# First two channel blocks multiplied one token stream at a time, and the last 512 output columns handled in halves

## The chip, the cores and the metric

One Trainium2 chip, one of its cores. The metric is the device time of the whole kernel in microseconds (us). Five engines work side by side, each through its own instructions in the order in which they stand: TensorE (PE in the rows; PEld is its weight load), VectorE (DVE), ScalarE (ACT), GpSimd (POOL) and SyncE (SP), which here only issues DMAs. They wait for each other through semaphores.

## The reference

Two layers of a token mixer with two streams of 256 tokens each and 1024 channels: the latent tokens `x`, and the context tokens `ctx`. Each layer has a gated FFN, a mixer and a second FFN; every one takes a modulated input and ends with a post-norm. Cut to what matters here:

```python
def _modulate(x, shift, scale):
    return _ln(x) * (1.0 + scale) + shift

def _swiglu(u, w_gate, w_up, w_down):
    return (jax.nn.silu(u @ w_gate) * (u @ w_up)) @ w_down
...
        mod = jax.nn.silu(c) @ w_mod[l] + b_mod[l]
        mod_c = jax.nn.silu(c_ctx) @ w_mod[l] + b_mod[l]
...
        h = _post_norm(h, 0.5 * m[2] * _swiglu(_modulate(h, m[0], m[1]), ...), ln_g[l, 0], ln_b[l, 0])
...
    return h
```

The output is the stream `h` of the latent tokens alone, after the last FFN of the second layer.

## The kernel before, in words

Tokens stand in four tiles of 128: tiles 0 and 1 are the first stream (latent tokens), tiles 2 and 3 the second (context tokens). Channels stand in eight blocks of 128, numbered `j`. Every matrix product is made in three passes of split float32 (`mm3`: high by high, high by low, low by high), so each weight tile has a part `whi` (cast by ScalarE, L68) and a part `wlo` (subtracted by VectorE, L69), and each input block has `uhi` and `ulo`.

The program begins in `run` with the first FFN of layer 0, whose first two weight tiles are multiplied while the inputs are still being made:

- `norm(t)` loads token tile `t`, takes its statistics on VectorE (`bn`, L190, and a few small instructions, one of them a power on GpSimd, L197) and normalises it on ScalarE into `xn` (L211).
- `mod_first(j)` loads the modulation weights of block `j` in two DMAs of 512 KB (`wm`, L112), multiplies them on TensorE in two halves of four matmuls (`pm`, L115; the trace counts each twice), copies the product on ScalarE (`msb`, L118), transposes it (`pmt`, L122), and VectorE makes shift and scale from it (`mred`, `modT`).
- `modulate_first(j)` transposes block `j` of all four token tiles (`put`, L134), applies shift and scale on ScalarE, one instruction a stream (`uv`, L138), and VectorE splits it into `uhi` (L140) and `ulo` (L141).
- `gate(j)` makes 12 matmuls of 512 columns (two weight tiles, gate and up, three passes), which add block `j` into four PSUM tiles. After `gate(7)` the same FFN goes on with its third weight tile.

A scheduler decides the order of each engine's instructions when the program is built; the order that it chose is fixed in the program. All these loads go through SyncE's one queue, in its order.

The program ends in `ffn(1, 1)` for the two tiles of the first stream. For its last 512 output columns, tile by tile: 33 matmuls (`pd`, eleven hidden blocks by three passes), `evac` on VectorE (multiply by the gate `ev` L259, add to `h` L264, statistics L190), and `boundary`: aggregate the statistics, the power on GpSimd (L197), subtract mean and scale (L275), scale and shift (L276), and one DMA of 512 KB to the output on SyncE's queue (L278).

Of the kernel before, what the change touches and what calls it, by code (L numbers as in the profile page):

```python
# [14 lines left out]
D = 1024  # L15
# [11 lines left out]
class Kernel:  # L27
# [45 lines left out]
    def mm3(self, ps, a, b, start, stop):  # L73
        """ps += a^T b, with a, b (high, low) pairs."""
        mm = self.nc.tensor.matmul
        mm(ps, a[0], b[0], start=start, stop=False)  # L76
        mm(ps, a[0], b[1], start=False, stop=False)  # L77
        mm(ps, a[1], b[0], start=False, stop=stop)  # L78

    # ---------------------------------------------------------------- set-up  # L80
# [24 lines left out]
    def mod_first(self, j, pool):  # L105
        """Shift and scale of model channels 128 j .. 128 j + 127 in the first sub-layer."""
# [22 lines left out]
    def modulate_first(self, j, pool, xn):  # L129
        """u of model channels 128 j .. 128 j + 127, all tokens."""  # L130
        nc = self.nc
        pt = self.psd.tile([128, 512], F32, name="put", tag="d")
        for t in range(4):
            nc.tensor.transpose(pt[:, 128 * t:128 * t + 128], xn[t][:, 128 * j:128 * j + 128], self.ident)  # L134
        v = pool.tile([128, 512], F32, name="uv", tag="uv", bufs=2)
        for s in range(2):
# [3 lines left out]
        nc.vector.tensor_copy(self.uhi[:, j], v)  # L140
        nc.vector.tensor_sub(self.ulo[:, j], v, self.uhi[:, j].bitcast(F32))  # L141
# [22 lines left out]
    def mod(self, l, n):  # L164
        """Columns 512 n .. 512 n + 511 of both streams' modulation vectors of layer l, 128 (on partitions) a step."""
# [19 lines left out]
    # ---------------------------------------------------------------- norms  # L185
    def bn(self, tt, ch):
        """Partial statistics of half a row of h."""
        if ch == 0 or tt not in self.bst:
            self.bst[tt] = self.sm.tile([128, 2, 6], F32, name="bst", tag="bst")
        self.nc.vector.bn_stats(self.bst[tt][:, ch], self.h[:, tt, 512 * ch:512 * ch + 512])  # L190

    def rsqrt(self, var, scale):
        """(var * scale + eps) ** -0.5"""
# [6 lines left out]
    def row_stats(self, tt):  # L200
        mv = self.sm.tile([128, 2], F32, name="mv", tag="mv")
        self.nc.vector.bn_aggr(mv, self.bst.pop(tt))
# [11 lines left out]
    def modulate(self, pool, l, slot, tt, xn, gs=(0, 1), dve=0):  # L214
        """u (feature-major, high and low) = xn (1 + scale) + shift for one token tile."""
# [20 lines left out]
    def load_gate(self, pool, l, gate, streams):  # L236
        """The gates of a sub-layer, on every partition."""
# [7 lines left out]
    def load_norm(self, pool, l, i):  # L245
        """Row vectors of a post-norm, on every partition."""
# [7 lines left out]
    def evac(self, pool, nrm, tt, ch, ps, first, final):  # L254
        """h += gate * ps on one half of the columns (h scaled by alpha at the first)."""
        nc = self.nc
        cs = slice(512 * ch, 512 * ch + 512)
        t = pool.tile([128, 512], F32, name="ev", tag="ev", bufs=2)
        nc.vector.tensor_mul(t, ps, nrm[TT_S[tt]][:, cs])  # L259
# [5 lines left out]
        if final:  # L265
            self.bn(tt, ch)

    def boundary(self, pool, nrm, tt, nxt):
        """h = LN(h) g + b; then the next sub-layer's modulated input, or the output."""
# [5 lines left out]
        nc.vector.scalar_tensor_tensor(xn, h, mu, nrm["g"], op0=OP.subtract, op1=OP.mult)  # L275
        nc.vector.scalar_tensor_tensor(h, xn, rs, nrm["b"], op0=OP.mult, op1=OP.add, accum_out=q[:, 0:1])  # L276
        if nxt is None:
            nc.sync.dma_start(self.out[128 * tt:128 * tt + 128], h)  # L278
            return
# [4 lines left out]
    # ---------------------------------------------------------------- FFN  # L284
    def ffn(self, l, f, tiles, nxt, mid, begun=None, post=()):
        """mid(stack): for each half of the hidden channels, streams (steps, from, to) to run in the places
        0 to 22 between the weight tiles; begun: the PSUM tiles of the first two weight tiles, if they are already done."""
# [3 lines left out]
        with ExitStack() as es:  # L291
# [6 lines left out]
            for fh in range(2):  # L298
# [29 lines left out]
                for ch in range(2):  # L328
# [5 lines left out]
                    def step(k, t):  # L334
                        i = tiles.index(t)
                        hi, lo = ws[k]
                        self.mm3(ps[t], (gt[k][:, 0, 128 * i:128 * i + 128], gt[k][:, 1, 128 * i:128 * i + 128]),
                                 (hi, lo), start=k == 0, stop=k == 10)
# [32 lines left out]
    def gate_load(self, l, f, ms, outer=False):  # L371
        """Weights (one pair per half of the model channels) and PSUM tiles of hidden tiles ms."""
# [19 lines left out]
    def gate_out(self, pool, PS, T):  # L392
        """silu(u w_gate) (u w_up), feature-major, high and low parts."""
# [948 lines left out]
```

## Time and profile before

| | |
|---|---|
| time, median of 3 runs | 2058.04 us (2054.61 to 2058.64) |
| span of the profiled execution | 2059.9 us, from the first to the last instruction |
| TensorE busy | 1980.4 us, 96% of the span |
| VectorE busy | 1519.5 us, 74% |
| ScalarE busy | 781.1 us, 38% |
| mean granted TensorE clock | 0.987 |

The profiled execution has no time of its own beside its span; the span is 1.9 us above the median of the three runs. Busy times are sums over the whole program, which has stages with different limits; the change touches only the first 60 us and the last 20 us, so these are read by themselves.

### The profile page before, as it was taken

To read this page: it belongs to the slowest core of one execution; us is meant where nothing else is said; L and a number is where in the kernel's file an instruction comes from. 1 tells how busy PE (TensorE), PEld (TensorE's weight loads), DVE (VectorE), ACT (ScalarE), POOL (GpSimd) and SP (SyncE) were. 2 spreads that over 40 slices of the span, in tenths; PEclk is the share of its full clock that TensorE was granted. 3 is DMA by queue.
4 is the path that set the end of the run, shared out by engine and by line. 5 is a ranking of instruction groups with operands and counts; after the bars stand their busy time and mean duration, and the time that the engine had idled before them with its cause. 6 is when DMAs were issued, how large, how long until landed. Compare 5 with 4: busy or idle time off the path is not lost. (4 is left out here: it accounts for less than half of the span.)

```text
span 2059.9 us, 28737 instructions
## 1 busy us (share of the span) xinstructions
PE 1980.4 (96%) x10556; PEld 1644.6 (80%) x10556; DVE 1519.5 (74%) x3352; ACT 781.1 (38%) x1300; POOL 157.0 (8%) x221
## 2 busy tenths in 40 slices
PE   7999999999999999999999989999998999979997
PEld 4888887787767887888888878888887877968896
DVE  4996998868996347766998767768778587684555
ACT  4321332345554224432233252312224566444442
POOL 0000110121100002200000030000003110010000
PEclk9999999999999999999999999999999999998999
DMA  8454566355344333345565525546552643564563
GB/s 312 154 152 143 184 202 215 118 178 163 120 147 133 101 103 123 113 148 180 184 197 186 187 97 188 166 158 198 173 183 88 188 156 117 163 232 136 182 188 112
DMA packets 103119, 333.10 MB, mean 162 GB/s; under 512 B 12353, under 2 KB 25505, under 8 KB 102977
## 3 DMA queue, kind: packets, MB, share of 16 engines
q1 hardware_dynamic: 96384, 310.96, 47.6%
q10 hardware_dynamic: 3584, 14.24, 1.8%
q0 software_dynamic: 3008, 6.07, 1.0%
q8 instruction: 83, 1.36, 0.3%
q14 instruction: 60, 0.48, 0.1%
HBM read 313.70 MB, written 17.51 MB: 161 GB/s over the span
## 5 line engine op out<-in xcount | busy, mean ns | idle before, releaser
L68 ACT CAST whi<-raw 128x1024 fp32r<-128x1024 f32 (+1 forms) x384 | 394.9, 1031 | 615.6 <-PE pd L78 160.2
L69 DVE TENSOR_TENSOR wlo<-raw,whi 128x1024 fp32r<-128x1024 f32 (+1 forms) x384 | 462.7, 1207 | 219.8 <-ACT whi L68 218.3
L178 DVE SCALAR_TENSOR_TENSOR pj<-raw,cb 128x512 f32<-128x512 f32 x512 | 351.7, 706 | 51.3 <-DMA raw<-in_w_modT 47.7
L76 PE MATMUL pg<-uhi,whi 128*128 128x512 f32 (+1 forms) x736 | 265.7, 361 | 1.6 <-DVE uhi L233 1.3
L78 PE MATMUL pg<-uhi,wlo 128*128 128x512 f32 (+1 forms) x736 | 263.1, 357 | 2.3 <-DVE wlo L69 2.3
L76 PE MATMUL pu<-uhi,whi 128*128 128x512 f32 (+1 forms) x736 | 263.2, 358 | 1.5 <-DVE ev L259 1.5
L77 PE MATMUL pg<-ulo,whi 128*128 128x512 f32 (+1 forms) x736 | 263.2, 358 | 0.6 <-POOL ulo L234 0.5
L77 PE MATMUL pu<-ulo,whi 128*128 128x512 f32 (+1 forms) x736 | 262.7, 357 | 0.0
L78 PE MATMUL pu<-uhi,wlo 128*128 128x512 f32 (+1 forms) x736 | 262.5, 357 | 0.0
L77 PE MATMUL pd<-wlo,gT 128*128 128x512 f32 x616 | 240.6, 391 | 1.6 <-DVE wlo L69 1.5
L76 PE MATMUL pd<-whi,gT 128*128 128x512 f32 x616 | 240.8, 391 | 0.9 <-DVE ev L259 0.9
L78 PE MATMUL pd<-whi,gT 128*128 128x512 f32 x616 | 239.5, 390 | 0.0
L76 PEld LDWEIGHTS pg<-uhi,whi 128*128 128x128 f32 x736 | 140.9, 191 | 26.1 <-issue 3.8
L78 PEld LDWEIGHTS pg<-uhi,wlo 128*128 128x128 f32 x736 | 140.7, 191 | 22.0 <-DVE wlo L69 2.7
L76 PEld LDWEIGHTS pu<-uhi,whi 128*128 128x128 f32 x736 | 140.9, 192 | 21.6 <-DVE ev L259 1.7
L77 PEld LDWEIGHTS pg<-ulo,whi 128*128 128x128 f32 x736 | 140.4, 191 | 20.9 <-POOL ulo L234 1.1
L77 PEld LDWEIGHTS pu<-ulo,whi 128*128 128x128 f32 x736 | 140.6, 191 | 20.2 <-issue 0.8
L78 PEld LDWEIGHTS pu<-uhi,wlo 128*128 128x128 f32 x736 | 140.5, 191 | 19.8 <-issue 0.4
L76 PEld LDWEIGHTS pd<-whi,gT 128*128 128x128 f32 x616 | 115.6, 188 | 27.2 <-issue 1.3
L77 PEld LDWEIGHTS pd<-wlo,gT 128*128 128x128 f32 x616 | 115.7, 188 | 25.9 <-DVE wlo L69 2.5
L78 PEld LDWEIGHTS pd<-whi,gT 128*128 128x128 f32 x616 | 115.7, 188 | 23.9
L76 PE MATMUL pgg<-uhi,whi 128*128 128x512 f32 (+1 forms) x384 | 131.8, 344 | 0.0
(561 smaller groups left out, 3234.0 us busy)
## 6 DMA issues: line engine op xcount, KB each, us to landing
raw<-in_w_gu SPq DMA_DIRECT2D x176, 512.0 KB
raw<-in_w_modT SPq DMA_DIRECT2D x128, 512.0 KB
raw<-in_w_dn SPq DMA_DIRECT2D x80, 512.0 KB
raw<-in_w_in SPq DMA_DIRECT2D x80, 512.0 KB
sd<-sst ACTq DMA_DIRECT2D x16, 802.0 KB
sst<-sd SPq DMA_DIRECT2D x16, 802.0 KB
wm<-in_w_mod SPq DMA_DIRECT2D x16, 512.0 KB
raw<-in_w_br SPq DMA_DIRECT2D x16, 512.0 KB
```

The lines of the kernel that those rows point to most:

```text
L68: nc.scalar.copy(hi[:, :m], raw[:, :m])
L69: nc.vector.tensor_sub(lo[:, :m], raw[:, :m], hi[:, :m].bitcast(F32))
L76: mm(ps, a[0], b[0], start=start, stop=False)
L77: mm(ps, a[0], b[1], start=False, stop=False)
L78: mm(ps, a[1], b[0], start=False, stop=stop)
L178: V.scalar_tensor_tensor(junk, raw[:, 512 * k:512 * k + 512], 1.0, self.cb[:, s, 512 * k:512 * k + 512], op0=OP.mult, op1=OP.mult, accum_o ...
```

## The change

At the start, `modulate_first` can work on one stream, and `gate` on half of the columns. Blocks 0 and 1 are made and multiplied for the first stream (256 columns) with only token tiles 0 and 1; the loads and norms of tiles 2 and 3 come after the first weight tiles and after the modulation weights of block 1; then blocks 0 and 1 are made and multiplied for the second stream, behind `begun`. From block 2 on all 512 columns go together, and the modulation of a block runs one block further ahead. At the end, the last token tile's last 512 columns are made in two halves of 33 matmuls of 256 columns each, each half is evacuated by itself, and every output tile is scaled and stored in two halves, the first on ScalarE's DMA queue and the second on SyncE's. Comments and docstrings are removed besides. The core of the diff:

```diff
-    def modulate_first(self, j, pool, xn):
+    def modulate_first(self, j, pool, xn, streams=(0, 1)):
...
-        v = pool.tile([128, 512], F32, name="uv", tag="uv", bufs=2)
-        for s in range(2):
+        v = pool.tile([128, 512], F32, name="uv", tag="uv", bufs=3)
+        for s in streams:
+            for t in range(2 * s, 2 * s + 2):
+                nc.tensor.transpose(pt[:, 128 * t:128 * t + 128], xn[t][:, 128 * j:128 * j + 128], self.ident)
...
         xn = pool.tile([128, D], F32, name="xn1", tag="xn", bufs=2)
...
+        if nxt is None:
+            for i, eng in enumerate((nc.scalar, nc.sync)):
+                cs = slice(512 * i, 512 * i + 512)
+                nc.vector.scalar_tensor_tensor(h[:, cs], xn[:, cs], rs, nrm["b"][:, cs], op0=OP.mult, op1=OP.add)
+                eng.dma_start(self.out[128 * tt:128 * tt + 128, cs], h[:, cs])
+            return
         nc.vector.scalar_tensor_tensor(h, xn, rs, nrm["b"], op0=OP.mult, op1=OP.add, accum_out=q[:, 0:1])
-        if nxt is None:
-            nc.sync.dma_start(self.out[128 * tt:128 * tt + 128], h)
-            return
...
                     for t in tiles:
-                        for k in range(11):
-                            step(k, t)
-                        self.evac(pool, nrm, t, ch, ps[t], False, True)
+                        if nxt is None and t == tiles[-1]:
+                            for i in range(2):
+                                for k in range(11):
+                                    step(k, t, 256 * i, 256 * i + 256)
+                                self.evac(pool, nrm, t, ch, ps[t], False, True, (i,))
+                        else:
+                            for k in range(11):
+                                step(k, t)
+                            self.evac(pool, nrm, t, ch, ps[t], False, True)
...
                 xn = [norm(t) for t in range(2)]
                 next(mod[0])
-                xn += [norm(t) for t in range(2, 4)]
                 next(mod[0], None)
-                self.modulate_first(0, pool, xn)
                 load(0)
                 next(mod[1])
+                self.modulate_first(0, pool, xn, (0,))
                 next(mod[1], None)
-                for j in range(KT):
-                    if j == 1:
-                        load(1)
-                    if j + 1 < KT:
-                        self.modulate_first(j + 1, pool, xn)
+                xn += [norm(t) for t in range(2, 4)]
+                begun = gate(0, 0, 256)
+                self.modulate_first(1, pool, xn, (0,))
+                next(mod[2])
+                gate(1, 0, 256)
+                next(mod[2], None)
+                for j in range(2):
+                    self.modulate_first(j, pool, xn, (1,))
+                for j in range(2):
+                    with self.tc.issue_after(begun):
+                        gate(j, 256, 512)
+                    self.modulate_first(j + 2, pool, xn)
+                    next(mod[j + 3])
+                    next(mod[j + 3], None)
+                load(1)
+                for j in range(2, KT):
...
```

Three places of the built programs, where the prediction's terms rest. Outside the first eight blocks and the last output columns every engine's order is the same in both.

ScalarE near the start, before: `xn` are the normalised token tiles (the first row holds tiles 0 and 1), `msb` the copied modulation products, `whi` weight casts, `uv` the modulated blocks.

```order
L211 ACTIVATE xn<-h,nb,nv 128x1024 x2
L118 COPY msb<-pm 128x256
L211 ACTIVATE xn<-h,nb,nv 128x1024
L68 CAST whi<-raw 128x1024
L211 ACTIVATE xn<-h,nb,nv 128x1024
L68 CAST whi<-raw 128x1024
L138 ACTIVATE uv<-put,modT 128x256 x2
L118 COPY msb<-pm 128x256
```

The same place now:

```order
L216 ACTIVATE xn<-h,nb,nv 128x1024 x2
L118 COPY msb<-pm 128x256
L68 CAST whi<-raw 128x1024 x2
L138 ACTIVATE uv<-put,modT 128x256
L118 COPY msb<-pm 128x256
L138 ACTIVATE uv<-put,modT 128x256
L216 ACTIVATE xn<-h,nb,nv 128x1024 x2
L118 COPY msb<-pm 128x256
L138 ACTIVATE uv<-put,modT 128x256 x4
```

The norms of tiles 2 and 3 moved behind the first stream's `uv` of blocks 0 and 1, and the copy `msb` of block 2 stands behind them.

VectorE near the start, before: `bst`, `mv`, `nv`, `nmu`, `nb` are a token tile's statistics, the last two norms (tiles 2 and 3) stand here.

```order
L190 BN_STATS bst<-h 128x6
L210 TENSOR_TENSOR nb<-nmu,nv 128x1
L190 BN_STATS bst<-h 128x6
L126 TENSOR_SCALAR modT<-mred,bmT 128x2
L202 BN_AGGR mv<-bst 128x2
L196 TENSOR_SCALAR nv<-mv 128x1
L1178 TENSOR_SCALAR nmu<-mv 128x1
L210 TENSOR_TENSOR nb<-nmu,nv 128x1
L69 TENSOR_TENSOR wlo<-raw,whi 128x1024 x2
L140 CAST uhi<-uv 128x512
L141 TENSOR_TENSOR ulo<-uv,uhi 128x512
```

The same place now, from the statistics of tile 2 on; `uhi` and `ulo` here are block 1 of the first stream:

```order
L192 BN_STATS bst<-h 128x6 x2
L141 CAST uhi<-uv 128x256
L207 BN_AGGR mv<-bst 128x2
L192 BN_STATS bst<-h 128x6
L200 TENSOR_SCALAR nv<-mv 128x1
L1193 TENSOR_SCALAR nmu<-mv 128x1
L192 BN_STATS bst<-h 128x6
L215 TENSOR_TENSOR nb<-nmu,nv 128x1
L142 TENSOR_TENSOR ulo<-uv,uhi 128x256
L207 BN_AGGR mv<-bst 128x2
L200 TENSOR_SCALAR nv<-mv 128x1
L1193 TENSOR_SCALAR nmu<-mv 128x1
```

The rest of both norms moved behind `uhi` of block 1, and between `uhi` and `ulo` of that block now stand eight instructions of the norms.

VectorE at the very end, before: the last token tile's evacuation and post-norm.

```order
L259 TENSOR_TENSOR ev<-pd,gbc_17304 128x512
L264 TENSOR_TENSOR h<-h,ev 128x512
L190 BN_STATS bst<-h 128x6
L202 BN_AGGR mv<-bst 128x2
L196 TENSOR_SCALAR nv<-mv 128x1
L275 SCALAR_TENSOR_TENSOR xn_18448<-h,mv,lng 128x1024
L276 SCALAR_TENSOR_TENSOR h,q<-xn_18448,nv,lnb 128x1024
```

The same place now:

```order
L265 TENSOR_TENSOR ev<-pd,gbc_17336 128x256
L270 TENSOR_TENSOR h<-h,ev 128x256
L192 BN_STATS bst<-h 128x6
L265 TENSOR_TENSOR ev<-pd,gbc_17336 128x256
L270 TENSOR_TENSOR h<-h,ev 128x256
L192 BN_STATS bst<-h 128x6
L207 BN_AGGR mv<-bst 128x2
L200 TENSOR_SCALAR nv<-mv 128x1
L281 SCALAR_TENSOR_TENSOR xn_18519<-h,mv,lng 128x1024
L285 SCALAR_TENSOR_TENSOR h<-xn_18519,nv,lnb 128x512 x2
```

Each instruction of the evacuation is there twice at half the width, and the last one of the post-norm is cut in two.

## Rows read from the trace of the kernel before

**Rows 1.** The page, busy time of the engine, share of the span, instructions.

```profile
PE 1980.4 (96%) x10556; PEld 1644.6 (80%) x10556; DVE 1519.5 (74%) x3352; ACT 781.1 (38%) x1300; POOL 157.0 (8%) x221
```

**Rows 2.** Timeline of TensorE, the start: start us, us, engine, line, operation, count.

```profile
18.09 1.94 PE L115 MATMUL pm<-wm,cTs 128*32 128x256 f32 x16
20.21 0.80 PE L76 MATMUL pg<-uhi,whi 128*128 128x512 f32 x1 [0.19 <-DVE uhi L140]
...
30.12 0.39 PE L76 MATMUL pg<-uhi,whi 128*128 128x512 f32 x1
30.35 0.39 PE L77 MATMUL pg<-ulo,whi 128*128 128x512 f32 x1
...
56.23 0.39 PE L76 MATMUL pg<-uhi,whi 128*128 128x512 f32 x1
```

**Rows 3.** Timeline of TensorE, one block's modulation among the products.

```profile
36.10 0.38 PE L122 MATMUL pmt<-ident,msb 128*128 128x128 f32 x2
...
36.85 0.64 PE L115 MATMUL pm<-wm,cTs 128*32 128x256 f32 x8
37.42 0.50 PE L77 MATMUL pg<-ulo,whi 128*128 128x512 f32 x1
37.76 0.39 PE L78 MATMUL pg<-uhi,wlo 128*128 128x512 f32 x1
```

**Rows 4.** Timeline of VectorE, the start.

```profile
6.22 1.29 DVE L190 BATCH_NORM_STATS2 bst<-h 128x6 f32<-128x512 f32 x2 [4.78 <-DMA h<-in_hx]
...
10.29 0.16 DVE L210 TENSOR_TENSOR nb<-nmu,nv 128x1 f32<-128x1 f32 x1 [0.60 <-POOL nv L197]
11.33 1.29 DVE L190 BATCH_NORM_STATS2 bst<-h 128x6 f32<-128x512 f32 x2 [0.89 <-DMA h<-in_hx]
```

**Rows 5.** Stretches 14 to 18 us: length, busy PE, PEld, DVE, ACT, POOL, PEclk, DMA, GB/s.

```profile
14.00:16.00 2.00, 0.39 (x1) 0.18 (x1) 1.36 (x8) 1.69 (x2) 0.63 (x2) 1.00 1.04 317
16.00:18.00 2.00, 0.40 (x2) 0.18 (x1) 1.36 (x2) 2.00 (x3) 0.00 (x0) 1.00 1.01 412
```

**Rows 6.** Groups of instructions, 0 to 60 us, by form: busy us, mean ns, idle before.

```profile
L138 ACT ACTIVATE uv<-put,modT 128x256 f32<-128x256 f32 x16 | 8.2, 560 | 12.3 <-DVE modT L126 12.3
...
L211 ACT ACTIVATE xn<-h,nb,nv 128x1024 f32<-128x1024 f32 x4 | 4.9, 1236 | 8.3 <-DVE nb L210 8.3
...
L118 ACT COPY msb<-pm 128x256 f32<-128x256 f32 x8 | 2.9, 369 | 6.3 <-PE pm L115 6.3
```

**Rows 7.** Timeline of TensorE, matmuls of 256 columns around a change of clock.

```profile
1864.27 0.41 PE L78 MATMUL pg<-uhi,wlo 128*128 128x256 f32 x1
1864.49 0.41 PE L76 MATMUL pu<-uhi,whi 128*128 128x256 f32 x1
...
1865.12 0.28 PE L77 MATMUL pg<-ulo,whi 128*128 128x256 f32 x1
1865.24 0.28 PE L78 MATMUL pg<-uhi,wlo 128*128 128x256 f32 x1
```

**Rows 8.** Timeline of VectorE, the end.

```profile
2049.41 0.69 DVE L259 TENSOR_TENSOR ev<-pd,gbc 128x512 f32<-128x512 f32 x1 [1.97 <-PE pd L78]
...
2050.86 0.69 DVE L190 BATCH_NORM_STATS2 bst<-h 128x6 f32<-128x512 f32 x1
...
2053.62 1.28 DVE L276 SCALAR_TENSOR_TENSOR h<-xn,nv,lnb 128x1024 f32<-128x1024 f32 x1 [0.44 <-POOL nv L197]
```

**Rows 9.** Timeline of GpSimd, the end.

```profile
2052.07 1.52 POOL L197 TENSOR_TENSOR nv<-nv,mhalf 128x1 f32<-128x1 f32 x1 [5.96 <-DVE nv L196]
```

**Rows 10.** Groups of instructions, 1975 to 2060 us, by form.

```profile
L398 DVE TENSOR_TENSOR sg<-sg,pu 128x256 f32<-128x256 f32 x8 | 3.4, 421 | 6.1 <-ACT sg L397 6.1
```

**Rows 11.** One stretch of the output's transfer, columns as in rows 5.

```profile
2056.00:2057.00 1.00, 0.00 (x0) 0.00 (x0) 0.00 (x0) 0.00 (x0) 0.00 (x0) 0.50 1.00 410
```

**Rows 12.** Two stretches with a fall of TensorE's clock, columns as in rows 5.

```profile
308.00:311.77 3.77, 1.59 (x7) 0.97 (x6) 3.77 (x11) 0.00 (x0) 1.03 (x2) 1.00 0.50 150
311.77:315.18 3.41, 3.32 (x8) 2.64 (x9) 3.27 (x10) 1.55 (x2) 0.00 (x0) 0.50 0.77 225
```

More of the change, by code (lines that the diff above doesn't have):

```diff
@@ L77, in mm3 @@
         mm(ps, a[0], b[1], start=False, stop=False)
-        mm(ps, a[1], b[0], start=False, stop=stop)
+        self.last = mm(ps, a[1], b[0], start=False, stop=stop)
     def setup(self, pool):
@@ L139, in modulate_first @@
                                  scale=self.modT[0][:, 8 + j, s:s + 1])
-        nc.vector.tensor_copy(self.uhi[:, j], v)
-        nc.vector.tensor_sub(self.ulo[:, j], v, self.uhi[:, j].bitcast(F32))
+        cs = slice(256 * streams[0], 256 * streams[-1] + 256)
+        nc.vector.tensor_copy(self.uhi[:, j, cs], v[:, cs])
+        nc.vector.tensor_sub(self.ulo[:, j, cs], v[:, cs], self.uhi[:, j, cs].bitcast(F32))
     def mod_out(self, l, n, res):
@@ L183, in mod, with bn @@
         self.mod_out(l, n, res[:, 0])
[L186 to L190, printed above, removed]
+    def bn(self, tt, ch, qs=(0, 1)):
+        if (ch == 0 and qs[0] == 0) or tt not in self.bst:
+            self.bst[tt] = [self.sm.tile([128, 4, 6], F32, name="bst", tag="bst"), 0]
+        st = self.bst[tt]
+        self.nc.vector.bn_stats(st[0][:, st[1]],
+                                self.h[:, tt, 512 * ch + 256 * qs[0]:512 * ch + 256 * qs[-1] + 256])
+        st[1] += 1
     def rsqrt(self, var, scale):
@@ L201, in row_stats @@
         mv = self.sm.tile([128, 2], F32, name="mv", tag="mv")
-        self.nc.vector.bn_aggr(mv, self.bst.pop(tt))
+        st, n = self.bst.pop(tt)
+        self.nc.vector.bn_aggr(mv, st[:, :n])
         return mv[:, 0:1], self.rsqrt(mv[:, 1:2], 1.0)
@@ L252, in load_norm, with evac @@
         return r
-    def evac(self, pool, nrm, tt, ch, ps, first, final):
+    def evac(self, pool, nrm, tt, ch, ps, first, final, qs=(0, 1)):
         nc = self.nc
-        cs = slice(512 * ch, 512 * ch + 512)
-        t = pool.tile([128, 512], F32, name="ev", tag="ev", bufs=2)
-        nc.vector.tensor_mul(t, ps, nrm[TT_S[tt]][:, cs])
+        cs = slice(512 * ch + 256 * qs[0], 512 * ch + 256 * qs[-1] + 256)
+        pc = slice(256 * qs[0], 256 * qs[-1] + 256)
+        t = pool.tile([128, 512], F32, name="ev", tag="ev", bufs=2)[:, pc]
+        nc.vector.tensor_mul(t, ps[:, pc], nrm[TT_S[tt]][:, cs])
         hh = self.h[:, tt, cs]
@@ L265, in evac @@
         if final:
-            self.bn(tt, ch)
+            self.bn(tt, ch, qs)
     def boundary(self, pool, nrm, tt, nxt):
@@ L332, in ffn, with step @@
                     ws = {}
-                    def step(k, t):
+                    def step(k, t, a=0, b=512):
                         i = tiles.index(t)
                         hi, lo = ws[k]
-                        self.mm3(ps[t], (gt[k][:, 0, 128 * i:128 * i + 128], gt[k][:, 1, 128 * i:128 * i + 128]),
-                                 (hi, lo), start=k == 0, stop=k == 10)
+                        self.mm3(ps[t][:, a:b], (gt[k][:, 0, 128 * i:128 * i + 128], gt[k][:, 1, 128 * i:128 * i + 128]),
+                                 (hi[:, a:b], lo[:, a:b]), start=k == 0, stop=k == 10)
                     for k0, n in ((0, 4), (4, 4), (8, 3)):
@@ L1186, in load, with gate @@
                         V[c, kh] = W[c, kh]()
-                def gate(j):
+                def gate(j, a=0, b=512):
                     for c in range(2):
@@ L1192, in gate @@
                             o = 512 * i + 128 * (j % 4)
-                            self.mm3(PS[c][i], (hi[:, o:o + 128], lo[:, o:o + 128]), (self.uhi[:, j], self.ulo[:, j]),
-                                     start=j == 0, stop=j == KT - 1)
+                            self.mm3(PS[c][i][:, a:b], (hi[:, o:o + 128], lo[:, o:o + 128]),
+                                     (self.uhi[:, j, a:b], self.ulo[:, j, a:b]), start=j == 0 and a == 0,
+                                     stop=j == KT - 1)
+                    return self.last.ins
                 mod = [self.mod_first(j, pool) for j in range(KT)]
@@ L1198, in run @@
                 next(mod[0])
-                xn += [norm(t) for t in range(2, 4)]
                 next(mod[0], None)
-                self.modulate_first(0, pool, xn)
                 load(0)
                 next(mod[1])
+                self.modulate_first(0, pool, xn, (0,))
                 next(mod[1], None)
-                for j in range(KT):
-                    if j == 1:
-                        load(1)
-                    if j + 1 < KT:
-                        self.modulate_first(j + 1, pool, xn)
+                xn += [norm(t) for t in range(2, 4)]
[14 more added lines that the diff above has]
+                for j in range(2, KT):
                     if j + 2 < KT:
-                        next(mod[j + 2])
+                        self.modulate_first(j + 2, pool, xn)
+                    if j + 3 < KT:
+                        next(mod[j + 3])
                     gate(j)
-                    if j + 2 < KT:
-                        next(mod[j + 2], None)
+                    if j + 3 < KT:
+                        next(mod[j + 3], None)
                 for i, n in enumerate(("c", "c_ctx")):
```

2 lines of the change are left out of this document (removed).

## The prediction
> **What bounds the kernel now.** I read the page's busy times first: TensorE works 96% of the span [rows 1], so time can be won only where it waits. The change touches two such places, the first 20 us and the last 10 us; in all the rest the order of every engine is unchanged. Then TensorE's timeline from the start: the first product stands at 20.21, waiting for `uhi`, and from there on the rows follow each other without idle time to 56.23, where the third weight tile begins [rows 2]. So before the change the first stage is: inputs until 20.2, then TensorE alone for 36 us. Third, VectorE's and GpSimd's timelines of the end: nothing else runs there, every instruction from 2049.41 on stands on the path [rows 8, 9], and the last DMA follows.
>
> The clock needs a word. The rows show PEclk 1.00 in the first stretches [rows 5], but 16 modulation matmuls took 1.94 us at 18.09 [rows 2] and 8 take 0.57 at 36.85 [rows 3]: 0.12 and 0.07 each. TensorE works at its lower level (1.2 GHz) at the start and at 2.4 GHz later, which stand side by side for 256 columns: 0.21 us apart before a change of clock, 0.12 after it [rows 7].
>
> **The start, step by step.** The loads come off one queue at one per 1.28 us: the first waits until 6.22, the fifth until 11.33 [rows 4]; around 15 us the rate falls from 412 to 317 GB/s for 2 us [rows 5], which is half a microsecond. The change puts the first weight tiles on places 5 and 6 and block 1's modulation weights on 7 and 8 (13.9 and 15.2), ahead of token tiles 2 and 3, which go to 9 and 10 (about 17 and 18.5). Block 2's stay on 11 and 12 (the last at about 21).
>
> Now TensorE's new order. Half of block 1's modulation from 13.9 takes 1.0 at the low clock, two transposes 0.5, `uv` 0.56 [rows 6], `uhi` about 0.3 (a 256-wide VectorE instruction takes 0.42 [rows 10], a cast less): the first product of the first stream starts at about 16.4 instead of 20.2. Twelve of them at 0.21 with a `pmt` between and a wait for `ulo` last to 19.6, or to 19.0 if the clock rises on the way. So far the change does what it says, and TensorE has 3.8 us more.
>
> These are not kept. Block 1 of the first stream needs transposes, `uv` and `uhi`, until 20.9 (20.0 with the higher clock). On VectorE, between this `uhi` and its `ulo`, now stand the aggregate of tile 2, both statistics of tile 3 (0.65 each, [rows 4]) and the wait for GpSimd's power (0.60 [rows 4]): with `ulo` itself 2.4 us, so TensorE's eight products with `ulo` start at 23.3 (22.4). Behind `ulo` come the aggregate of tile 3, its power and `nb`, 1.2 us, then on ScalarE `xn` of tile 3, 1.24, and only behind it `msb` of block 2, 0.37 [rows 6]. Its transpose `pmt` is next in TensorE's order, at P = 26.1 (25.2), although block 2's own modulation was done about 1.1 us earlier; TensorE idles for that long, and 0.7 to 0.9 us twice before.
>
> From P on TensorE has all it needs. Up to the first 512-wide product of block 2: 24 products of 256 at 0.12, 2.9; modulation of blocks 3 and 4, four halves of 0.57, 2.3 [rows 3]; two `pmt` 0.4; twelve transposes 1.1 (`pmt` and four transposes take 0.75 before a modulation half, [rows 3]); seven changes between kinds of matmul, about 0.1 to 0.17 each (37.42 to 37.76 is 0.34 where 0.23 is the beat, [rows 2, 3]), 0.9; a wait of 0.2 for `uhi` of the second stream: 7.9. After it: 72 products of 512 at 0.23, 16.6; six modulation halves of 0.77 with their changes, four `pmt`, eight pairs of transposes in places of their own. Before, the same 72 products and three halves, one `pmt` and one set of transposes more took 30.12 to 56.23, 26.1 us [rows 2]; 9.5 of that is not products. Less 3 x 0.77 and 0.66, plus 1.0 for transposes and halves standing apart now, it is 7.5. Sum: third weight tile at P + 7.9 + 24.1 = P + 32.0, so P = 24.2 would be no change. With 26.1 and 25.2 the start loses 1.9 or 1.0 us; I take **+1.4**, between them, since which one holds depends only on when the clock rises. Bounds: P can't be earlier than block 2's weights allow, 21.0 + 0.57 + 0.37, about 22, which gains 2.3; and a clock that falls again costs as in the second rival, up to +4.1.
>
> The third `uv` buffer, the missing comments and the extra argument cost nothing: no engine's order outside these two places is another. `issue_after` adds no wait that TensorE's order doesn't have.
>
> **The end.** The last tile's 33 products of 512 become 66 of 256: 66 x 0.12 - 33 x 0.23 = 7.92 - 7.59 = +0.35. Rounding of the rows leaves 0.25 to 0.45. The Trainium skill's "TensorE: Matmul & The Clock Gate", section "Wait — 56ns, not 53.3ns?", gives a start-to-start time of N columns / 2.4 GHz plus 2.5 ns; worked out from it the cut costs 66 x 0.1092 - 33 x 0.2158 = 0.09 (an estimate). By that rule the end would be 0.26 better than mine; the rows' beat is the slower one, and the sum keeps it.
>
> Against it, the first half's evacuation hides under the second half's products: the three instructions for `ev`, `h` and statistics, 0.72 each (two take from 2049.41 to 2050.86, [rows 8]), become three of about 0.44 (0.42 for a 256-wide instruction [rows 10]): -0.85. The power of 1.52 [rows 9] stays. Scale and shift, 1.28 [rows 8], become two halves that end together where it ended; the store behind the second is 0.26 MB instead of 0.52, at 410 GB/s [rows 11] 0.64 less, and the first half's store runs under the second's scale and shift: -0.6. The new ScalarE DMA waits behind nothing. Sum of the end: +0.35 - 0.85 - 0.6 = **-1.1**; from +0.4, if neither cut brings anything (evacuation waiting for both halves, store bound by its fixed part), to -1.6.
>
> **Sum.** +1.4 - 1.1 = +0.3. The profiled span of 2059.9 would become 2060.2; it stands 1.9 above the median of the runs, and carried to that median the time is **2058.3 us**. A difference under about 0.2% (4.1 us) is not to be told from no change; the three runs shown spread over 4.0 themselves.
>
> **The rivals.**
>
> First, the queue on VectorE is shorter than I make it (statistics of tiles 2 and 3 done before `uhi` of block 1 is due, so that P is set by block 2's weights). For it: both token tiles have landed by about 18.5. Against: `uhi` stands ahead of half of them in the fixed order. Start -2.3, end -1.1: **2054.6**, still within 0.2%, at its edge.
>
> Second, slower: TensorE's clock falls again, or rises late, in the gaps of 0.7, 0.9 and 1.1 us between 19 and 26. In the trace a stretch with 1.59 of 3.77 us busy was followed by one at 0.50 [rows 12]; in the new order I count some 3 of 6.4 busy there. From P on TensorE is the bound, and each microsecond at the low level loses half: one such stretch of 3.41 costs 1.7, and the low clock ahead of P 0.5 to 1, so **2061**. It decides the verdict (over +4.1) if the low clock lasts some 7.6 us beyond P, to about 33.7: 2062.2 and more. Against it: before, TensorE had also idled much until 18, and its products at 30.12 stood 0.23 apart, at the higher level [rows 2]. The Trainium skill's page just named, section "HAM oscillation — how this bites in real kernels", has this as a rule: gaps between bursts send the array back to its low clock, and each burst starts cold. By that rule this rival holds; the trace agrees that it happens in this kernel [rows 12].
>
> Third, later low-clock stretches like that of [rows 12] fall otherwise in the new runs, whatever the change does; two of them more or less are 3.4 us. Nothing in the change speaks for a direction: **2055 to 2062**.
>
> **How the numbers follow.** My sum 0.50; first rival 0.17, of which 0.03 beyond -4.1; second 0.20, of which 0.08 beyond +4.1; third 0.13, of which 0.07 faster and 0.03 slower. That is faster 0.10, slower 0.11, same 0.79. The range leaves out the parts of the rivals beyond the threshold and a little more: 2054.8 to 2061.8. The likeliest case alone has 2057.3 to 2059.3.
>
> **What would show it.** In the changed kernel's trace: first 256-wide product near 16.4; `ulo` of block 1 about 2.4 us behind its `uhi`; `msb` of block 2 straight behind `xn` of tile 3 and its `pmt` at 25 to 26; the third weight tile at 57 to 58 instead of 56.2; at the end `ev` of the last half about 0.35 later than 2049.4 plus the shift of the start, and about 3.4 us from that `ev` to scale and shift instead of 4.2 [rows 8]. If the third weight tile starts before 55, VectorE's queue was not the limit; if 256-wide products after P stand 0.21 apart, the second rival holds. The prediction is wrong if the whole moves by more than 4 us, which no step of mine reaches.

## The result, and the profile after

The changed kernel takes 2071.1 us (median of 4 runs, 2066.88 to 2073.33) where the kernel before, beside it, takes 2058.34. The ratio is 1.0066, interval 1.0053 to 1.0078: 13.6 us slower, 11 to 16. The prediction was 2058.3 with a range to 2061.8.

The profiled execution has a span of 2071.6 us. The page's row of busy times, after:

```profile
PE 1994.5 (96%) x10613; PEld 1652.6 (80%) x10613; DVE 1520.8 (73%) x3359; ACT 781.9 (38%) x1300; POOL 155.9 (8%) x221
```

TensorE is busy 14 us longer than in [rows 1]. It has 57 more records, 24 at the start and 33 at the end where products were cut in halves, and waits no longer in all, so its own work took longer. TensorE's timeline at the start, after:

```profile
16.87 0.58 PE L76 MATMUL pg<-uhi,whi 128*128 128x256 f32 x1
...
21.88 0.58 PE L76 MATMUL pg<-uhi,whi 128*128 128x256 f32 x1 [0.98 <-DVE uhi L141]
...
27.68 0.69 PE L122 MATMUL pmt<-ident,msb 128*128 128x128 f32 x2 [0.55 <-ACT msb L118]
...
31.61 0.41 PE L77 MATMUL pg<-ulo,whi 128*128 128x256 f32 x1
...
32.12 0.28 PE L78 MATMUL pu<-uhi,wlo 128*128 128x256 f32 x1
...
62.10 0.39 PE L76 MATMUL pg<-uhi,whi 128*128 128x512 f32 x1
```

The first product came at 16.87, as forecast (16.4). But TensorE ran at its lower level until about 31.8 (matmuls of 256 columns last 0.41, as in the upper rows of [rows 7], then 0.28). The third weight tile starts at 62.10 where it started at 56.23 [rows 2]: 5.9 us are gone here.

VectorE's timeline at the end, after:

```profile
2051.67 0.69 DVE L265 TENSOR_TENSOR ev<-pd,gbc 128x512 f32<-128x512 f32 x1 [2.82 <-PE pd L78]
...
2055.88 1.42 DVE L285 SCALAR_TENSOR_TENSOR h<-xn,nv,lnb 128x512 f32<-128x512 f32 x2 [0.44 <-POOL nv L201]
2057.21 0.42 DVE L265 TENSOR_TENSOR ev<-pd,gbc 128x256 f32<-128x256 f32 x1
...
2061.89 0.42 DVE L265 TENSOR_TENSOR ev<-pd,gbc 128x256 f32<-128x256 f32 x1 [3.33 <-PE pd L78]
...
2065.33 1.42 DVE L285 SCALAR_TENSOR_TENSOR h<-xn,nv,lnb 128x512 f32<-128x512 f32 x2 [0.44 <-POOL nv L201]
```

and TensorE's between the two halves of the last 512 columns:

```profile
2055.26 0.28 PE L78 MATMUL pd<-whi,gT 128*128 128x256 f32 x1
2057.69 0.38 PE L76 MATMUL pd<-whi,gT 128*128 128x256 f32 x1 [2.15 <-DVE ev L265]
```

The row of before that belongs beside them, the evacuation of the first token tile:

```profile
2041.93 0.69 DVE L259 TENSOR_TENSOR ev<-pd,gbc 128x512 f32<-128x512 f32 x1 [2.73 <-PE pd L78]
```

The second half's first product waits 2.15 us for the `ev` of the first half at 2057.21, which stands on VectorE behind the first tile's post-norm (its scale and shift begin at 2055.88). From the first tile's `ev` to the last half's it was 2049.41 - 2041.93 = 7.48 us [rows 8]; now it is 2061.89 - 2051.67 = 10.22, so 2.7 more. From the last `ev` to scale and shift: 4.21 before, 3.44 now. From there to the end of the span: 2059.9 - 2053.62 = 6.28 before [rows 8], 2071.6 - 2065.33 = 6.27 now, though the store is in halves. The end costs 2.0 us.

These two places make 7.9 us. In between, one stretch stood out, in the second layer's mixer, where the order is the same. Two windows after, columns as in [rows 5]:

```profile
1648.00:1653.30 5.30, 3.14 (x25) 2.84 (x23) 2.20 (x4) 3.20 (x7) 0.76 (x2) 1.00 0.54 187
1653.30:1663.50 10.20, 10.20 (x44) 7.97 (x45) 5.06 (x14) 4.72 (x9) 2.06 (x5) 0.50 0.42 145
```

TensorE was busy 3.14 of 5.30 us, and then worked 10.2 us at half clock. Whether that belonged to the change was the first question.

### The profile page after: what moved, and what is told of

The parts are those of the page before. It is cut to its first block, busy times and chain, and to the rows that moved or that the text cites. A ratio compares the mean times of both kernels' runs of the same rounds, so it can differ in the third digit from the quotient of the medians.

```text
span 2071.6 us, 28861 instructions
## 1 busy us (share of the span) xinstructions
PE 1994.5 (96%) x10613; PEld 1652.6 (80%) x10613; DVE 1520.8 (73%) x3359; ACT 781.9 (38%) x1300; POOL 155.9 (8%) x221
## 5 line engine op out<-in xcount | busy, mean ns | idle before, releaser
L76 PE MATMUL pd<-whi,gT 128*128 128x512 f32 (+1 forms) x627 | 244.5, 390 | 2.8 <-DVE ev L265 2.8
L77 PE MATMUL pd<-wlo,gT 128*128 128x512 f32 (+1 forms) x627 | 243.2, 388 | 0.0
L78 PE MATMUL pd<-whi,gT 128*128 128x512 f32 (+1 forms) x627 | 242.6, 388 | 0.0
L77 PEld LDWEIGHTS pu<-ulo,whi 128*128 128x128 f32 x740 | 141.5, 191 | 19.8 <-issue 0.4
L76 PEld LDWEIGHTS pd<-whi,gT 128*128 128x128 f32 x627 | 117.8, 188 | 29.4 <-DVE ev L265 3.4
L78 PEld LDWEIGHTS pd<-whi,gT 128*128 128x128 f32 x627 | 117.8, 188 | 25.2
```

The source lines that it names most:

```text
L78: self.last = mm(ps, a[1], b[0], start=False, stop=stop)
```

## The experiments

The theory was: late clock at the start, a wait at the end, and chance in the mixer. The rivals: the mixer's loss follows from the change, or the start loses by VectorE's order rather than by the clock. The first four kernels take the change apart.

**Start alone** (the end as before):

```diff
-                        if nxt is None and t == tiles[-1]:
...
-            for i, eng in enumerate((nc.scalar, nc.sync)):
...
+            nc.sync.dma_start(self.out[128 * tt:128 * tt + 128], h)
```

> The change at the start alone; the end is that of the kernel before. Read from the two traces, the products behind the start stand 4.8 to 5.0 us later, the second mixer adds 4.7 and the end 2.0. If the loss in the second mixer (a transfer of 7.30 us where 5.95 stood, then 10.2 us at half clock) falls there by chance, this kernel is 5 us slower than before, ratio about 1.0024, and no such stretch stands near 1650. If the shift of the start brings it about, it is 9 to 10 us slower, ratio about 1.0047, with the stretch. If the start costs nothing beyond its first 60 us and the records of the clock mislead, it is as before.

Measured: 1.0039, interval 1.0028 to 1.0049, 8 us, with no half clock near 1650. Neither account holds: the time is nearer to the dearer one, but without the stretch that was to explain it.

**End alone** (the functions of the start as before):

```diff
-                gate(1, 0, 256)
...
+                for j in range(KT):
+                    if j == 1:
+                        load(1)
```

> The change at the end alone; the start is that of the kernel before. If the halves make the second half's first product wait for the first half's evacuation (2.15 us in the changed kernel), the end costs 2.0 us and the ratio is about 1.001. If the second mixer's loss belongs to what the end's code does to the program (buffers, queues), it is 6.7 us slower, ratio about 1.0033, and the slow transfer stands near 1645 again. By the prediction it would be 1.1 us faster.

Measured: 1.0037, 1.0026 to 1.0049, also 8 us. By the medians the parts cost 8.3 and 8.4 us and the whole 12.8, so they seem to share something of about 4 (by the ratios 2.0, each uncertain by some 2). Both carry one edit that is no instruction: `bst`, the tile of a token's statistics, grew from `[128, 2, 6]` to `[128, 4, 6]`, in six buffers, each 32 bytes larger as it is laid out. In the built programs every SBUF tile made after it stands 192 bytes further on.

**Filling gaps at the start.** Transposes of data already at hand, into columns of a PSUM tile that are overwritten later; their result is not used. Four of them:

```diff
+            if first and j:
+                for t in range(4):
+                    nc.tensor.transpose(pt[:, 384:512], xn[0][:, 0:128], self.ident)
```

> The start alone, with four more transposes on TensorE (into a part of a PSUM tile that is overwritten later) where it waited 0.98 us for the first stream's second block at 21.9. They make nothing that is used. If the start loses because TensorE stays at its low level through gaps, filling the largest gap lets the clock rise one step earlier or more: matmuls of 256 columns 0.12 apart from about 25 instead of 31.8, and the third weight tile 1.5 to 3 us earlier than with the start alone. If the loss is the order on VectorE and ScalarE, the extra transposes change nothing or cost up to 1 us.

and eight more behind block 0's `pmt`:

```diff
+            for i in range(8):
+                nc.tensor.transpose(self.pt0[:, 384:512], sb[:, 0:128], self.ident)
```

> The start alone, with eight more transposes between block 0's first transposes and its products and four ahead of block 1's products; by them the scheduler also sets block 0's first products ahead of block 1's modulation. They make nothing that is used. If the clock is the cause, TensorE has nearly no gap from 12 to 21 and rises by about 20: the third weight tile starts at 57 or earlier where the changed kernel has about 61. If VectorE's order is the cause, the third weight tile stays within 1 us of the start alone.

Measured: 2063.3 and 2066.29 us (one run each). The third weight tile in TensorE's timeline, with four:

```profile
59.39 0.39 PE L76 MATMUL pg<-uhi,whi 128*128 128x512 f32 x1
```

and with twelve:

```profile
60.71 0.39 PE L76 MATMUL pg<-uhi,whi 128*128 128x512 f32 x1
```

The start alone, unfilled, has it earlier than both:

```profile
58.52 0.39 PE L76 MATMUL pg<-uhi,whi 128*128 128x512 f32 x1
```

The extra work pays nothing. The start alone already had the higher level from 19.8 on, and with four transposes it came at 19.5; so a late clock is not what this run loses by. Twelve transposes are no clean test: the clock rose at 15.8, but fell again from 22.6 to 26.0 (columns as in [rows 5]):

```profile
22.60:26.00 3.40, 3.40 (x19) 2.36 (x19) 2.09 (x10) 1.88 (x2) 1.09 (x2) 0.50 1.02 407
```

**The statistics tile alone**, in the kernel before:

```diff
-            self.bst[tt] = self.sm.tile([128, 2, 6], F32, name="bst", tag="bst")
+            self.bst[tt] = self.sm.tile([128, 4, 6], F32, name="bst", tag="bst")
...
-        self.nc.vector.bn_aggr(mv, self.bst.pop(tt))
+        self.nc.vector.bn_aggr(mv, self.bst.pop(tt)[:, 0:2])
```

> The kernel before with one thing of the change: the tile of a token's statistics has room for four partial results instead of two (six buffers, so every tile made after it in SBUF stands 192 bytes further on). Same instructions, same order. The start alone and the end alone each cost 8.3 to 8.4 us while both together cost 12.7, and each carries this tile: if it costs the common 4 us by where the tiles stand, this kernel is 3.5 to 5 us slower, ratio about 1.002. If the time beyond the start and the end is chance or follows from the shift in time, it is as before, ratio 1.000.

Measured: 1.0019, 1.0008 to 1.0029, that is 3.9 us. Not one instruction differs. Where it goes is seen in a stretch of 132 products of `gT` in the first FFN's last pass, which follow each other without a wait, so that their step from start to start (the beat) can be read: first and last in TensorE's timeline, before

```profile
347.76 0.39 PE L76 MATMUL pd<-whi,gT 128*128 128x512 f32 x1
...
377.46 0.39 PE L78 MATMUL pd<-whi,gT 128*128 128x512 f32 x1
```

and with the larger statistics tile

```profile
347.12 0.39 PE L76 MATMUL pd<-whi,gT 128*128 128x512 f32 x1
...
377.10 0.39 PE L78 MATMUL pd<-whi,gT 128*128 128x512 f32 x1
```

29.70 us against 29.98 for 131 steps. The program has 1848 such products, 14 times this stretch: 14 x 0.28 = 3.9 us. The 192 products of 512 columns that read a moved `bh` (last section) add an estimated 192 x 6.2 ns = 1.2 us. Together that is 5.1, within the 1.6 to 6.0 of the interval.

**The place varied**, by an unused tile in the kernel before:

```diff
+        self.sm.tile([128, 16], F32, name="pad", tag="pad", bufs=1)
```

(64 bytes; 128 with `[128, 32]`.)

> The kernel before with an unused tile of 64 bytes ahead of the token statistics: all tiles made after stand 64 bytes further on. Nothing else differs. In undisturbed stretches of the profiles with the tiles moved by 192 bytes, the products that read a moved tile stand further apart (products with gT 229.3 ns instead of 227.1, those with bh 233.4 instead of 227.2), those that read none stay at 226.8. If the place is what costs, 64 bytes give some other beat for gT and bh and leave the products of uhi alone; if the larger statistics tile cost in another way, the beats are those of before.

> The same with 128 bytes. Counted from a multiple of 128, the moved tiles then stand where they stood before (96), with 64 or 192 bytes they stand at 32. If the beat goes by that, this kernel has the beats of before (227.1 and 227.2) and 64 bytes have those of the changed kernel (229.3 and 233.4).

Measured: 2071.32 and 2063.03 us, one run each beside one of 2057.55 before. The same stretch with 64 bytes

```profile
349.71 0.40 PE L76 MATMUL pd<-whi,gT 128*128 128x512 f32 x1
...
380.28 0.40 PE L78 MATMUL pd<-whi,gT 128*128 128x512 f32 x1
```

and with 128

```profile
348.06 0.40 PE L76 MATMUL pd<-whi,gT 128*128 128x512 f32 x1
...
378.50 0.40 PE L78 MATMUL pd<-whi,gT 128*128 128x512 f32 x1
```

30.57 and 30.44 us: 233.4 and 232.4 ns a product, where before has 226.7 and 192 bytes give 228.9. My guess that a multiple of 128 decides is refuted by the second. 14 x 0.87 = 12.2 us is what the first should lose by this, and it lost 13.8; 14 x 0.74 = 10.4 for the second, which lost 5.5 in its one run. The kernel before alone scatters from 2053 to 2064 us in its runs, so two single runs say little about such sums; the beats are what this experiment shows.

Then everything at even places, by 32 bytes ahead of the first large tiles, and by 256 more ahead of the statistics:

```diff
+        C.tile([128, 8], F32, name="pad")
...
+        self.sm.tile([128, 64], F32, name="pad", tag="pad", bufs=1)
```

> The kernel before with an unused tile of 32 bytes among the first constants: all later tiles, uhi and the weights too, then stand at multiples of 256 bytes. If a tile that begins off a multiple of 64 or 128 costs TensorE something in each read, all beats fall below 226.8, and every nanosecond is worth some 10 us over the kernel; if 226.8 is not set by that, nothing moves.

> The same, with 256 bytes more ahead of the token statistics: gT, bh and yT stand at multiples of 512 bytes too. Against the kernel with 32 bytes this tells whether 512 matters: the beats of gT and bh move or stay.

Measured: 2061.31 and 2056.06 us, one run each. The stretch with 32 bytes:

```profile
347.73 0.39 PE L76 MATMUL pd<-whi,gT 128*128 128x512 f32 x1
...
377.42 0.39 PE L78 MATMUL pd<-whi,gT 128*128 128x512 f32 x1
```

29.69 us: nothing is won over the kernel before, and 512 instead of 256 changes nothing either (345.78 to 375.47). The kernel with 32 bytes also shows that the mixer's slow stretch needs no part of the change, a window of it:

```profile
1646.30:1653.10 6.80, 6.80 (x31) 4.72 (x30) 4.07 (x11) 4.72 (x9) 1.30 (x4) 0.50 0.59 214
```

Such a stretch near 1650 stands in 7 of the 18 profiles, here with neither part of the change.

**The whole change, tiles at their old places:** the last tile takes its larger statistics from a pool made at the end.

```diff
+            self.bst[tt] = [big.tile([128, 4, 6], F32, name="bsl", tag="bsl") if big else
+                            self.sm.tile([128, 2, 6], F32, name="bst", tag="bst"), 0]
```

> The changed kernel with the old tile for the statistics; only the last token tile takes a larger one, from a pool that is made at the end, so that every other tile stands where it stood before. If the place of the tiles costs 4 to 5 us, this is 4 to 5 us faster than the changed kernel: ratio to before about 1.004 instead of 1.0066. If not, 1.006 to 1.007 again.

Measured: 1.0059, 1.0046 to 1.0072, in 5 runs. That is nearer to the second case of the expectation than to the first, and the interval overlaps that of the changed kernel (1.0053 to 1.0078). By itself it settles nothing.

**The end alone, last half in a PSUM tile of its own**, tiles at their old places:

```diff
                             for i in range(2):
+                                if i:
+                                    ps[t] = self.psd.tile([128, 512], F32, name="pd", tag="d")
```

> The change at the end alone, with the last half in a PSUM tile of its own, and the tiles where they stood before; the start is that of before. If the second half waited for the first half's evacuation because both lie in one PSUM tile, the wait of 2.15 us is gone, the last evacuation starts at most 0.4 us later than before the change counted from the first token tile's, scale and shift start 3.4 us behind it instead of 4.2, and the end is 0.3 to 0.5 us faster than before: ratio 0.999 to 1.001. If the wait is of another kind (VectorE's order), it stays, and the end costs 2 us, ratio 1.001.

Measured: 0.9994, 0.9982 to 1.0006. TensorE between the halves, and VectorE's `ev` of the first tile, of the last half, and scale and shift:

```profile
2045.07 0.28 PE L78 MATMUL pd<-whi,gT 128*128 128x256 f32 x1
2045.19 0.28 PE L76 MATMUL pd<-whi,gT 128*128 128x256 f32 x1
```

```profile
2041.44 0.69 DVE L265 TENSOR_TENSOR ev<-pd,gbc 128x512 f32<-128x512 f32 x1 [2.87 <-PE pd L78]
...
2049.34 0.42 DVE L265 TENSOR_TENSOR ev<-pd,gbc 128x256 f32<-128x256 f32 x1 [1.02 <-PE pd L78]
...
2052.78 1.41 DVE L285 SCALAR_TENSOR_TENSOR h<-xn,nv,lnb 128x512 f32<-128x512 f32 x2 [0.44 <-POOL nv L201]
```

(The last token tile's statistics are those of the kernel just told.) The halves follow each other at 0.12, the wait is gone, though the first half's `ev` still stands behind the first tile's norm (scale and shift from 2045.66, `ev` at 2046.99). It was the shared PSUM tile. What the halves then bring: 7.90 instead of 7.48 up to the last `ev`, 3.44 instead of 4.21 behind it, 2059.0 - 2052.78 = 6.22 to the end: 0.3 to 0.4 us. The halved store brings nothing, although its transfer ends sooner. The last window with traffic, before and then here (columns as in [rows 5]):

```profile
2057.00:2057.50 0.50, 0.00 (x0) 0.00 (x0) 0.00 (x0) 0.00 (x0) 0.00 (x0) 0.50 0.12 41
```

```profile
2055.50:2056.00 0.50, 0.00 (x0) 0.00 (x0) 0.00 (x0) 0.00 (x0) 0.00 (x0) 0.50 0.64 238
```

Counted from the start of scale and shift the transfer ends at about 3.6 us before and 3.2 here, but the span ends at 6.2 in both. What sets that end is not shown.

**The changed kernel once more:**

> The changed kernel once more, for a second profile. In the profiles so far the clock first rises at 21.6 before, 31.9 in the changed kernel and 19.8 with the start alone, which has the same order there. If the late rise belongs to the order, it is near 30 again and the products behind the start stand 5 us later than before; if it depends on how the run falls, it may come near 20, and the start then costs 2 to 2.5 us. The stretch at half clock near 1653 comes again only if it is not chance.

Measured: 2066.59 us, no half clock near 1650, and the higher level from 20.0 on. Block 2's `pmt` and the third weight tile, then the second half's first product, and a window behind it:

```profile
26.73 0.44 PE L122 MATMUL pmt<-ident,msb 128*128 128x128 f32 x2 [0.88 <-ACT msb L118]
...
59.30 0.39 PE L76 MATMUL pg<-uhi,whi 128*128 128x512 f32 x1
...
2049.41 0.38 PE L76 MATMUL pd<-whi,gT 128*128 128x256 f32 x1 [2.14 <-DVE ev L265]
```

```profile
2051.00:2054.40 3.40, 3.40 (x18) 3.40 (x18) 0.00 (x0) 0.00 (x0) 0.00 (x0) 0.50 0.00 0
```

So the same program's clock rises at 20.0 in one run and at 31.9 in another. And the wait at the end has a second price that the first profile lacked: TensorE waits 2.14 us, its clock falls to 0.50, and the products of that window run at half speed. The last `ev` then comes 11.75 us behind the first tile's (2055.15 - 2043.40), where it was 7.48 before and 10.22 in the first profile. In four of the five profiles with the unmended end the clock falls like this.

**Each part by itself at the old places** was still open. For the start alone the edit is the one below, beside that of the start alone above; for the end, unmended, and for the whole change with the end mended it is the pool of its own for the last statistics, told above.

```diff
-            self.bst[tt] = [self.sm.tile([128, 4, 6], F32, name="bst", tag="bst"), 0]
+            self.bst[tt] = [self.sm.tile([128, 2, 6], F32, name="bst", tag="bst"), 0]
```

> The change at the start alone, all tiles of the later stages at their old places. If the start costs only what stands in its first 60 us, 2.4 to 3.2 us with a clock that rises near 20 and 6 with one that rises near 32, this is 3 to 4 us slower than before: ratio 1.0013 to 1.002. If the start also disturbs what follows, 7 to 8 us, ratio 1.0035 to 1.004.

> The change at the end alone with the wait between the halves, tiles at their old places. If the wait of 2.15 us and the half clock that followed it in three of four profiles are its whole cost, it is 2 to 3.6 us slower: ratio 1.001 to 1.0018. With the tiles moved it was 1.0037. If the tiles' place did nothing there, 1.0037 again.

> The whole change with the last half in a PSUM tile of its own and the tiles at their old places. If start, end and place add up, only the start is left: 1.0012 to 1.002, the same as the start alone less 0.3 us. If both together cost what neither does, it is nearer 1.004 to 1.006.

Measured: start alone 1.0019 (1.0008 to 1.0031), end alone, unmended, 1.002 (1.0008 to 1.0031), both with the end mended 1.003 (1.0019 to 1.0042). In us: 4, 4 and 6, each uncertain by some 2.4. The first two are as expected or just above; the third lies above its 1.0012 to 1.002, though its interval reaches down to that. The start alone, `pmt` of block 2, its first product of 512 columns and the third weight tile:

```profile
25.91 0.44 PE L122 MATMUL pmt<-ident,msb 128*128 128x128 f32 x2 [0.88 <-ACT msb L118]
...
34.36 0.50 PE L76 MATMUL pg<-uhi,whi 128*128 128x512 f32 x1
...
58.41 0.39 PE L76 MATMUL pg<-uhi,whi 128*128 128x512 f32 x1
```

and on ScalarE `xn` of tile 3 with the copy `msb` of block 2 straight behind it:

```profile
24.36 1.24 ACT L216 ACTIVATE xn<-h,nb,nv 128x1024 f32<-128x1024 f32 x1 [0.22 <-DVE nb L215]
25.50 0.35 ACT L118 COPY msb<-pm 128x256 f32<-128x256 f32 x1
```

In the ten profiles with the old start the third weight tile stands at 55.9 to 57.1, in the six with the new one and nothing added at 58.4 to 59.3, and once, in the first, at 62.1.

The profiles show one thing more of the three kernels that have the new start and the old places (the start alone, and the whole change with the end unmended and mended). All three have the slow stretch near 1650, and a fall of the clock near 388 that none of the other 15 has. In the start alone:

```profile
383.00:387.70 4.70, 2.30 (x11) 1.56 (x9) 4.70 (x9) 0.00 (x0) 0.00 (x0) 1.00 0.42 128
387.70:391.10 3.40, 2.89 (x7) 2.31 (x8) 3.30 (x6) 0.00 (x0) 0.00 (x0) 0.51 0.51 139
```

Between 60 and 2040 us these three spend 44 to 48 us at half clock, the others 34 to 51 with a median of 41. Half of the difference, 2 to 3 us, is about what they lie above the sums below. With one profile each this is a hint, not shown.

**The version that the runs point to:** the start of before, the end in halves with its own PSUM tile, everything at multiples of 512 bytes.

> The start of before, the end in halves with a PSUM tile of its own, and the tiles at multiples of 512 bytes. The end gives 0.2 to 0.3 us and the place nothing to 2 us (one run at multiples of 512 was 1.5 us below its partner, with the beats of before): ratio 0.998 to 1.000.

Measured: 1.0, 0.9989 to 1.0011. It beats nothing: the 0.3 to 0.4 us of the end are below what the runs can tell.

## Why the prediction was wrong

Three causes, timed one by one: start 4, end 4, place of the tiles 3.9, together 12 where 13.6 (11 to 16) was measured. The traces price them at 2.2 to 3.1 (5.9 with a late clock), 2.0 to 3.5 and 5.1. The 1 to 2 us by which the timed start exceeds its trace lie within the uncertainty. In twos they do not add up so well. The whole change at the old places should cost the 8 us of start and end, and cost 12 (1.0059); with the end mended it should cost 4, and cost 6. The first excess is about as large as the uncertainties taken together. The five runs of that kernel also had a lower clock, 0.986 in the mean where the 23 beside them of the kernel before had 0.988. That is 4 to 5 us, of which the fall at the end takes 1.7. Whether that is chance, or start and end together bring about falls of the clock elsewhere, stays open.

**The step that failed outright** is "cost nothing: no engine's order outside these two places is another". The order was indeed the same, and I took it for the time. The diff's `[128, 4, 6]` moved every later tile by 192 bytes, and products that read a moved `gT` went from 226.7 to 228.9 ns. I did not name `bst` in the costs at all. So the change did not touch only the first 60 us and the last 20, as I had written ahead of the prediction; by that term alone the kernel before lost 3.9 us, which I had put at nothing.

**The end.** The step "the first half's evacuation hides under the second half's products" held the halves for independent. They share a PSUM tile, and the second half's first product waited for VectorE's read of the first: +2.0 us in the first profile, and with the fall of the clock 11.75 - 7.48 - 0.77 = 3.5. My upper bound of +0.4 assumed a late evacuation, not a waiting TensorE. The other terms, measured where the wait is gone: the 66 products +0.42 (forecast +0.35), the halved evacuation -0.77 (forecast -0.85), the halved store 0 (forecast -0.6; from scale and shift to the end 6.2 to 6.3 with and without it, though the transfer itself ended 0.4 sooner). So even the mended end is worth 0.3, not 1.1. The Trainium skill's "TensorE: Matmul & The Clock Gate", section "Wait — 56ns, not 53.3ns?", would make the 66 products 0.09 longer by my estimate. The runs show 0.42, so the rows' beat was the better guide.

**The start.** The mechanism was right, the size a little short. VectorE's and ScalarE's queues set block 2's `pmt`: 25.9 in four of the later profiles, forecast 25.2 to 26.1, and 26.73 in one whose first product came about 1 us later. `msb` stands straight behind `xn` of tile 3, as forecast, and the wait of 0.88 for it is near the 1.1 that I gave it. From there the third weight tile took 32.5 us, forecast 32.0. The term that was too small is the 7.9 up to the first product of block 2 with 512 columns: it took 8.45 (34.36 - 25.91), and its parts as I listed them add to 7.8. The 24.1 behind it held (24.05). That is +2.2 to +3.1 instead of +1.4. In one of the six profiles with this order and nothing added, the clock rose at 31.9, and it was +5.9: the second rival, to which I gave 0.20 and 2061. Its condition for a slower verdict, a low clock to about 33.7, nearly came true in that one run, but a late rise was not the main cause: in the other five the clock rose by 20.0, and they lose 2 to 3 us all the same. For the start the runs show that one order can fall on either side; what decides it is not shown. The Trainium skill's "TensorE: Matmul & The Clock Gate", section "HAM oscillation — how this bites in real kernels", describes waits between bursts of products after which the next burst starts at the low clock. Those waits are longer than the gaps of about 1 us at the start, so my "By that rule this rival holds" read the page too widely. At the end this case shows the like (2.14 us of waiting, then 0.50).

**The first rival** (a short queue on VectorE, 2054.6) is refuted by `pmt` at 25.91, where I had put it at about 22 for this case. **The third** (stretches that fall otherwise) held as far as it went: the stretch near 1650 comes and goes, also without the change, and made the first profile look as if 4.7 us were lost in the mixer. Whether the change makes it more frequent is not shown.

## What to carry to other kernels

An edit that leaves every instruction and its order alone can still cost, because a larger tile moves all that are made after it: compare the tiles' places as well as the order, and compare the beat of undisturbed products in both traces. Two halves of one PSUM tile were not independent of each other here; give the second its own tile if the first is to be read while the second is written, and count the clock's fall with the wait. One profile is one draw: here the first one showed a late clock and a slow stretch that a second one did not.

## What the hardware showed unasked

The step from one matmul to the next changed with the place in SBUF where an operand begins. In the built programs `gT`, loaded as weights, begins 224 bytes past a multiple of 256 in the kernel before: 226.7 ns. At 0 (the kernel with 32 bytes) it is 226.6, at 160 it is 228.9, at 96 232.4, at 32 233.4. The streamed operand `bh` in the mixer's merge shows it too. First and last of 22 products without a wait, before

```profile
723.46 0.39 PE L76 MATMUL pdb<-bh,whi 128*128 128x512 f32 x1
...
728.22 0.39 PE L76 MATMUL pdb<-bh,whi 128*128 128x512 f32 x1
```

and in the changed kernel

```profile
727.61 0.39 PE L76 MATMUL pdb<-bh,whi 128*128 128x512 f32 x1
...
732.50 0.40 PE L76 MATMUL pdb<-bh,whi 128*128 128x512 f32 x1
```

that is 226.7 against 232.9 ns. `uhi` was not moved by the 192 bytes, and its products keep the beat of before (227.3 and 227.2 ns, the mean over the whole program). One reading is not separated from this one: with 192, 64 and 128 bytes only one of the two operands of a product moved, while the 32 bytes moved both alike. So it can be the distance between the two operands that counts, and not the place of one. Why these places and not others cost was not tried further.
